# Two-layer trunk on one core: head transposes as SBUF-to-SBUF block moves and a VectorE block transpose, in place of TensorE transposes

## The chip, the cores and the metric

The kernel runs on one core of a Trainium2 chip. The metric is the device time of one execution in microseconds (us), the median of three runs.

## The reference, cut to what matters

The residual stream x has 256 positions of 2048 values, in float32. Two layers are computed one after the other.

```
even layer: h = rms_norm(x); proj = h @ w_in               # 2048 -> 32 heads x (q, k, v, gate) x 128
  heads 0-15  (stick-breaking): z = q k^T / sqrt(128), strict causal mask;
              A = exp(log_sigmoid(z) + reverse cumulative sum of log_sigmoid(-z));  o = A v
  heads 16-31 (dilated): q, k rms-normed per head; three dilated causal softmaxes merged;  o = P v
  x = x + (o * silu(gate)) @ w_out                         # 4096 -> 2048
odd layer: h = rms_norm(x); proj = h @ w_in                # 32 heads x (q, forget, input, gate) x 128
  HGRN2 per head: S_t = diag(f_t) S_{t-1} + (1 - f_t) i_t^T;  o_t = S_t^T q_t
  x = x + (rms_norm(o) * silu(gate)) @ w_out
```

In the score product of a head, and in the output product that takes up the gated outputs (`mix`), the 128 values of a head are summed over. TensorE sums over partitions, so queries, keys and `mix`, which come out with positions on partitions, have to be turned.

## The kernel before, in words

Each of the 64 heads is a product of the 256 positions with 2048 x 512 weights (128 columns each of q, k, v and gate). `product` runs over 16 steps of 128 rows; a step is six matmuls of 128x512 (two halves of the positions, and three terms each: high part of x times high part of the weights, high times low, low times high; lines L254 to L256). Two steps share one weight pair: `Feed.load` (L200) brings 512 KB into one of four buffers `raw`, ScalarE casts it to the high part `whi` (L211), VectorE subtracts to get the low part `wlo` (L212). `whi` and `wlo` have four buffers each, so a head takes eight pairs, and up to four pairs can stand split ahead of TensorE (`AHEAD`). After a layer's 32 heads, four output products of 32 steps read the turned `mixh` and `mixl` in the same way.

The work of a head behind its product is a generator (`stick_breaking`, `dilated` or `hgrn`). `Side.tick` moves the generators on once per step of the next heads' products; a `yield n` means "go on n steps later". So side work of one head lies between the matmuls of the next two. A tile scheduler then places all of this into one fixed order per engine. It may put an instruction later than the source has it when its own estimate says that the inputs are not there yet. Each engine, and the queue of SyncE (SP) that issues the transfers, runs its list strictly in order.

The generator starts with `evacuate` (L275): ScalarE copies the two 128x512 accumulators out of PSUM, scaled. These copies have to wait for the last matmul of the head. `flip` (L137) turns 128x128 blocks on TensorE against an identity matrix, into PSUM: four per head for queries and keys (`flip_pair`), two for the gated outputs (`emit_mix`), and three for attention weights in the even layer (`flip_weights`, not changed). In `emit_mix`, `split_into` (L128, L129) writes the turned `mixh` and `mixl` straight from PSUM.

Of the kernel before, what the change touches and what calls it, by code (L numbers as in the profile page):

```python
# [18 lines left out]
P = 128  # L19
# [15 lines left out]
def hybrid_trunk(  # L35
# [34 lines left out]
    ones = const.tile([P, SEQ], F32, name="ones")  # L70
    nc.vector.memset(ones, 1.0)
# [68 lines left out]
    def flip_pair(pj):  # L140

        ps = flip([pj[:, t, c * P : (c + 1) * P] for c in range(2) for t in range(NT)])
        return ps.rearrange("p (c t) -> p c t", c=2)
# [134 lines left out]
    def gate_exp(pj):  # L278

        g = pj[:, :, 384:512]  # L280
# [14 lines left out]
    def weighted_values(at0, at1, at11, pj, c):  # L295


        o = psb.tile([P, NT, P], F32, name="att")
        v = pj[:, :, c * P : (c + 1) * P]
        nc.tensor.matmul(o[:, 0, :], at0, v[:, 0, :], start=True, stop=True)  # L300
        nc.tensor.matmul(o[:, 1, :], at1, v[:, 0, :], start=True, stop=False)  # L301
        nc.tensor.matmul(o[:, 1, :], at11, v[:, 1, :], start=False, stop=True)  # L302
        return o

    def stick_breaking(h, pj):
        sg = gate_exp(pj)
        yield 4
        ps = flip_pair(pj)
        qk = work.tile([P, 2, SEQ], F32, name="qk", bufs=2)
        nc.scalar.copy(qk, ps)  # L310
        yield 3
        zp = psb.tile([P, 384], F32, name="att")
        nc.tensor.matmul(zp[:, 0:128], qk[:, 0, 0:P], qk[:, 1, 0:P], start=True, stop=True)  # L313
        nc.tensor.matmul(zp[:, 128:384], qk[:, 0, P:], qk[:, 1, :], start=True, stop=True)  # L314
# [10 lines left out]
        for lo, hi in ((0, 128), (128, 384)):  # L325
            back = sp[:, lo:hi][:, ::-1]
            nc.vector.tensor_tensor_scan(back, ones[:, 0 : hi - lo], back, 0.0, ALU.mult, ALU.add)
# [5 lines left out]
        o = weighted_values(at[:, 0:128], at[:, 128:256], at[:, 256:384], pj, 2)  # L333
        nc.vector.tensor_mul(sg, o, sg)
        yield 2
        emit_mix(h, sg, 1.0)

    def dilated(h, pj):
        sg = gate_exp(pj)
        qv = pj[:, :, 0:256].rearrange("p t (c d) -> p t c d", c=2)  # L340
# [7 lines left out]
        for t in range(NT):  # L348
            sl = pj[:, t, P : 2 * P]
# [7 lines left out]
        z = psb.tile([P, 384], F32, name="att")  # L357
        nc.tensor.matmul(z[:, 0:128], qk[:, 0, 0:P], qk[:, 1, 0:P], start=True, stop=True)  # L358
        nc.tensor.matmul(z[:, 128:384], qk[:, 0, P:], qk[:, 1, :], start=True, stop=True)  # L359
# [22 lines left out]
        o = weighted_values(at[:, 0:128], at[:, 128:256], at[:, 256:384], pj, 2)  # L382
# [5 lines left out]
        emit_mix(h, sg, 1.0)  # L388

    def hgrn(h, pj):  # L390
        g = pj[:, :, 384:512]
# [8 lines left out]
        nc.scalar.activation(f, fp, AF.Sigmoid)  # L400
# [3 lines left out]
        nc.scalar.activation(kk, fp, AF.Sigmoid, scale=-1.0)  # L404
        q = work.tile([P, SEQ], F32, name="qt", bufs=2)
        nc.scalar.copy(q, ps[:, 0, :])
        nc.scalar.activation(kk, kk, AF.Copy, scale=oml[:, h : h + 1])

        def blocks(a, n):
            return a.rearrange("p (b n) -> p b n", n=n)  # L410
# [24 lines left out]
        nc.vector.tensor_mul(qb, q, qb)  # L435
# [7 lines left out]
        nc.vector.tensor_mul(qq, q, f)  # L443
# [77 lines left out]
        o = weighted_values(at[:, 0, :], cross, at[:, 1, :], pj, 2)  # L521
# [14 lines left out]
        emit_mix(h, sg, hg[:, 2:3])  # L536
# [13 lines left out]
    def head(layer, h, acc):  # L550
        pj = evacuate(acc, rstds[layer])
        if layer == 1:
            yield from hgrn(h, pj)
        elif h < NSB:
            yield from stick_breaking(h, pj)
        else:
            yield from dilated(h, pj)
# [143 lines left out]
```

## Time and profile before

| quantity | value |
|---|---|
| median of three runs | 1967.46 us (1967.27 to 1967.49) |
| profiled execution, its own time | 1967.47 us |
| its span on the core | 1965.7 us |
| TensorE busy | 1956.2 us (100%) |
| VectorE busy | 1286.5 us (65%) |
| ScalarE busy | 1038.3 us (53%) |
| DMA, share of 16 engines | 54%, 175 GB/s in the mean |
| granted TensorE clock | 1.00 |

The span is what the trace covers; the time of the profiled execution is 1.8 us longer. Busy time of TensorE counts a pipelined matmul to its modelled end, so two matmuls overlap in it: a 128x512 matmul shows 0.39 us, but the next one starts 0.23 us after it.

### The profile page before, as it was taken

Reading aid. Unit: us, or ns where it says so; the run is one execution under the profiler, and the core shown is the slowest. Engines: PE = TensorE matmul, PEld = TensorE weight load, DVE = VectorE, ACT = ScalarE, POOL = GpSimd, SP = SyncE. Lnnn points to the kernel's source line nnn. Section 1 sums busy time; section 2 is a strip of 40 time slices with the busy share of each in tenths; the row PEclk is TensorE's granted clock in tenths of the full one; section 3 lists DMA queues with packets and bytes.
Section 4 is the critical chain, followed back from the end, with each engine's and each line's share of the span. In section 5 each row is a group of like instructions: output and inputs, shape, how many; then the busy total and the mean of one; then the engine's idle time right before and its main releaser. Section 6 shows DMA issues by size and latency. Waiting matters only on the chain.

```text
span 1965.7 us, 25693 instructions
## 1 busy us (share of the span) xinstructions
PE 1956.2 (100%) x9280; PEld 1611.5 (82%) x9280; DVE 1286.5 (65%) x2456; ACT 1038.3 (53%) x1653; POOL 55.9 (3%) x54
## 2 busy tenths in 40 slices
PE   8999999999999999999999999999999999999999
PEld 7888888888888888888888888888888888888887
DVE  6666666666666666555577777777777777776444
ACT  6555555555555555444455555555555555555432
POOL 0000000000000000000000000000000000000000
PEclk9999999999999999999999999999999999999999
DMA  9555555555555555555554544555555544455664
GB/s 324 166 178 175 173 174 177 173 172 175 177 173 173 175 176 172 181 183 192 187 177 161 162 160 161 172 161 165 166 163 162 165 162 160 158 169 164 200 204 139
DMA packets 97407, 344.39 MB, mean 175 GB/s; under 512 B 11136, under 2 KB 12288, under 8 KB 97280
## 3 DMA queue, kind: packets, MB, share of 16 engines
q1 hardware_dynamic: 97136, 342.73, 54.0%
q8 instruction: 73, 1.20, 0.2%
q14 instruction: 54, 0.44, 0.1%
q10 hardware_dynamic: 144, 0.02, 0.0%
HBM read 340.61 MB, written 2.10 MB: 174 GB/s over the span
## 4 chain that ended last, share of the span: by engine, by line
PE 100%; DMA 0%; ACT 0%; DVE 0%; DVEq 0%; issue 0%
PE acc L254 30%; PE acc L256 30%; PE acc L255 30%; PE att L137 3%; PE att L461 2%; PE att L490 1%; PE att L301 1%; PE att L302 1%; PE att L300 1%; PE att L518 0%; PE att L359 0%; PE att L314 0%; DMA gn<-in_gains 0%; PE att L313 0%; PE att L358 0%; ACT xh L128 0%
## 5 line engine op out<-in xcount | busy, mean ns | idle before, releaser
L212 DVE TENSOR_TENSOR wlo<-raw,whi 128x1024 fp32r<-128x1024 f32 (+1 forms) x642 | 782.2, 1219 | 545.2 <-ACT whi L211 543.8
L211 ACT CAST whi<-raw 128x1024 fp32r<-128x1024 f32 (+1 forms) x642 | 673.2, 1049 | 631.6 <-PE acc L256 547.2
L254 PE MATMUL acc<-whi,xh 128*128 128x512 f32 x2048 | 837.4, 409 | 5.8 <-ACT whi L211 5.8
L256 PE MATMUL acc<-whi,xl 128*128 128x512 f32 x2048 | 802.6, 392 | 0.0
L255 PE MATMUL acc<-wlo,xh 128*128 128x512 f32 x2048 | 800.1, 391 | 0.0
L256 PEld LDWEIGHTS acc<-whi,xl 128*128 128x128 f32 x2048 | 384.9, 188 | 84.9
L254 PEld LDWEIGHTS acc<-whi,xh 128*128 128x128 f32 x2048 | 385.7, 188 | 79.0 <-ACT whi L211 5.8
L255 PEld LDWEIGHTS acc<-wlo,xh 128*128 128x128 f32 x2048 | 386.3, 189 | 72.0 <-DVE wlo L212 0.6
L254 PE MATMUL acc<-whi,mixh 128*128 128x512 f32 x512 | 201.8, 394 | 0.0
L256 PE MATMUL acc<-whi,mixl 128*128 128x512 f32 x512 | 199.5, 390 | 0.0
L255 PE MATMUL acc<-wlo,mixh 128*128 128x512 f32 x512 | 199.3, 389 | 0.0
L256 PEld LDWEIGHTS acc<-whi,mixl 128*128 128x128 f32 x512 | 96.1, 188 | 20.3
L255 PEld LDWEIGHTS acc<-wlo,mixh 128*128 128x128 f32 x512 | 96.2, 188 | 19.4
L254 PEld LDWEIGHTS acc<-whi,mixh 128*128 128x128 f32 x512 | 96.2, 188 | 19.3
L275 ACT ACTIVATE pj<-acc,rstd 128x512 f32<-128x512 f32 x128 | 87.5, 685 | 30.6 <-PE acc L256 30.1
L285 DVE RECIPROCAL sg<-sg 128x256 f32<-128x256 f32 x32 | 56.0, 1749 | 0.5
L179 POOL TENSOR_TENSOR rr<-rv,mhalf 128x4 f32<-128x4 f32 x16 | 29.3, 1833 | 716.0 <-DVE rv L178 716.0
L179 POOL TENSOR_TENSOR ro<-rv,mhalf 128x2 f32<-128x2 f32 x32 | 25.0, 780 | 831.0 <-DVE pr L474 808.0
L504 ACT COPY ri<-qk 128x128 f32<-128x128 f32 x32 | 9.6, 299 | 58.4 <-DVE qk L413 58.4
L137 PE MATMUL att<-ident,pj 128*128 128x128 f32 x256 | 38.5, 272 | 0.0
L413 DVE TENSOR_TENSOR qk<-qk 128x128 f32<-128x128 f32 x128 | 37.0, 289 | 2.2
L429 DVE RECIPROCAL ri<-qk 128x160 f32<-128x160 f32 x32 | 36.7, 1148 | 0.0
(141 smaller groups left out, 1272.3 us busy)
## 6 DMA issues: line engine op xcount, KB each, us to landing
raw<-in_w_odd SPq DMA_DIRECT2D x256, 512.0 KB, 3.6
raw<-in_w_even SPq DMA_DIRECT2D x254, 512.0 KB, 3.5
raw<-in_w_out SPq DMA_DIRECT2D x128, 512.0 KB, 3.5
xres<-in_xt SPq DMA_DIRECT2D x8, 256.0 KB, 7.3
xres<-in_x SPq DMA_DIRECT2D x4, 512.0 KB, 7.3
out<-xres SPq DMA_DIRECT2D x6, 256.0 KB, 5.1
raw<-in_w_even SPq DMA_DIRECT2D x4, 256.0 KB, 4.8
out<-xres SPq DMA_DIRECT2D x4, 128.0 KB, 2.0
```

The source lines that it names most:

```text
L137: nc.tensor.transpose(ps[:, i * P : (i + 1) * P], b, ident)
L179: nc.gpsimd.tensor_tensor(dst, v[:, 0:n], mhalf[:, 0:n], op=ALU.pow)
L211: nc.scalar.copy(hi[:, s, :], half[:, s, :])
L212: nc.vector.tensor_sub(lo[:, s, :], half[:, s, :], hi[:, s, :].bitcast(F32))
L254: nc.tensor.matmul(acc[t], sh[:, k, s], hi, start=(k == 0), stop=False)
L255: nc.tensor.matmul(acc[t], sh[:, k, s], lo, start=False, stop=False)
L256: nc.tensor.matmul(acc[t], sl[:, k, s], hi, start=False, stop=(k == nk - 1))
L275: nc.scalar.activation(pj[:, t, :], acc[t], AF.Copy, scale=rstd[:, t : t + 1])
L285: nc.vector.reciprocal(sg, sg)
L413: nc.vector.tensor_tensor(o, a, b.broadcast_to(list(o.shape)), op=ALU.mult)
L429: nc.vector.reciprocal(ri, f8[:, :, 3:8])
L461: nc.tensor.matmul(ps[:, t, :], kt[:, t * P : (t + 1) * P], qt[t], start=True, stop=True)
```

## The change

Queries and keys are evacuated into a tile of their own (`qkp`), values and gate into another (`pj`), with four 128x256 ScalarE instructions in place of two of 128x512. For all but the last head of a layer, `move_blocks` copies the tile to a second one (`mvp`, or `mvm` for `mix`) with 16 SBUF-to-SBUF transfers on SP's queue, one for each pair of 32-partition groups; 32x32 blocks change place, in runs of 128 bytes. Then one VectorE instruction (`turn_blocks`, STREAM_TRANSPOSE) turns each 32x32 block, back into the tile it came from. Between the two stands a `yield 4`. The last head of a layer keeps the TensorE transposes (of `qkp` with a copy from PSUM). The score products read `qkp` (`products`), the dilated head scales k in place, HGRN reads q and forget from SBUF, and `split_into` reads `mix` from SBUF. The scan in `stick_breaking` reads a broadcast column instead of a 128x256 tile of ones.

```
+    def move_blocks(src, name):
+        n = src.shape[2] // P
+        moved = work.tile([P, NT, n, 4, 32], F32, name=name, bufs=1)
+        to = moved.rearrange("p t c a j -> p (t c) a j")
+        v = src.rearrange("p t (c f) -> p (t c) f", f=P)
+        for a in range(4):
+            for b in range(4):
+                nc.sync.dma_start(
+                    to[32 * b : 32 * b + 32, :, a, :], v[32 * a : 32 * a + 32, :, 32 * b : 32 * b + 32]
+                )
+        return moved
+    def turn_blocks(dst, moved):
+        nc.vector.transpose(dst, moved.rearrange("p t c a j -> p (t c a j)"))
+    def turn_pair(qk, quick):
+        if quick:
+            ps = flip([qk[:, t, c * P : (c + 1) * P] for t in range(NT) for c in range(2)])
+            nc.scalar.copy(qk, ps.rearrange("p (t f) -> p t f", t=NT))
+        else:
+            moved = move_blocks(qk, "mvp")
+            yield 4
+            turn_blocks(qk.rearrange("p t f -> p (t f)"), moved)
...
     def evacuate(acc, rstd):
-        pj = work.tile([P, NT, 512], F32, name="pj", bufs=2)
-        for t in range(NT):
-            nc.scalar.activation(pj[:, t, :], acc[t], AF.Copy, scale=rstd[:, t : t + 1])
-        return pj
+        qk = work.tile([P, NT, 256], F32, name="qkp", bufs=2)
+        vg = work.tile([P, NT, 256], F32, name="pj", bufs=2)
+        for dst, c in ((qk, 0), (vg, 256)):
+            for t in range(NT):
+                nc.scalar.activation(
+                    dst[:, t, :], acc[t][:, c : c + 256], AF.Copy, scale=rstd[:, t : t + 1]
+                )
+        return qk, vg
...
     def emit_mix(h, mix, scale):
+        if h == NH - 1:
+            turned = flip([mix[:, t, :] for t in range(NT)])
+        else:
+            moved = move_blocks(mix, "mvm")
+            yield 4
+            turned = mix.rearrange("p t f -> p (t f)")
+            turn_blocks(turned, moved)
         mixed.append(h)
-        split_into(mixh[:, h, :], mixl[:, h, :], flip([mix[:, t, :] for t in range(NT)]), scale)
+        split_into(mixh[:, h, :], mixl[:, h, :], turned, scale)
...
-    def stick_breaking(h, pj):
-        sg = gate_exp(pj)
-        yield 4
-        ps = flip_pair(pj)
-        qk = work.tile([P, 2, SEQ], F32, name="qk", bufs=2)
-        nc.scalar.copy(qk, ps)
+    def stick_breaking(h, qk, vg):
+        sg = gate_exp(vg)
+        yield 2
+        yield from turn_pair(qk, False)
         yield 3
...
-        yield 8
-        ps = flip_pair(pj)
-        qk = work.tile([P, 2, SEQ], F32, name="qk", bufs=2)
-        nc.scalar.copy(qk[:, 0, :], ps[:, 0, :])
-        nc.scalar.activation(qk[:, 1, :], ps[:, 1, :], AF.Copy, scale=qkg)
+        yield 5
+        yield from turn_pair(qk, h == NH - 1)
+        k = qk[:, :, P:]
+        nc.scalar.activation(k, k, AF.Copy, scale=qkg)
         yield 3
...
-        yield 3
-        ps = flip_pair(pj)
-        fp = ps[:, 1, :]
+        yield 2
+        yield from turn_pair(qk, h == NH - 1)
+        q, fp = qk[:, :, 0:P], qk[:, :, P:]
```

The scheduler's order around the new instructions differs from the order before at many places. Three of them are shown, with the buffer numbers of the tiles, since they tell which head a row belongs to. The new file has other line numbers: the cast is L234 there, the low part L235, the evacuation L300, the gate L309 to L313, the turn L155.

First place, the end of a stick-breaking head's product. ScalarE before, where `acc_751` and `acc_752` are the finished head's accumulators, and `whi_891` (a row ahead of these), `whi_909` and `whi_927` the next head's first three weight pairs:

```order
L211 CAST whi_909<-raw_804 128x1024
L211 CAST whi_927<-raw_829 128x1024
L275 ACTIVATE pj_957<-acc_751,rstd0_429 128x512
L211 CAST whi_947<-raw_866 128x1024
L275 ACTIVATE pj_957<-acc_752,rstd0_429 128x512
L283 ACTIVATE sg_960<-sg_960 128x256
L211 CAST whi_974<-raw_889 128x1024
```

ScalarE now, where `acc_1236` and `acc_1237` are the finished head's accumulators, `whi_1348` is its last pair, `whi_1385` the next head's first pair and `whi_1420` its second:

```order
L234 CAST whi_1348<-raw_1238 128x1024
L234 CAST whi_1385<-raw_1268 128x1024
L300 ACTIVATE qkp_1471<-acc_1236,rstd0_429 128x256
L300 ACTIVATE pj_1472<-acc_1236,rstd0_429 128x256
L300 ACTIVATE qkp_1471<-acc_1237,rstd0_429 128x256
L300 ACTIVATE pj_1472<-acc_1237,rstd0_429 128x256
L310 ACTIVATE sg_1477<-sg_1477 128x256
L234 CAST whi_1420<-raw_1303 128x1024
```

Before, three pairs of the next head are cast ahead of the first copy out of the finished accumulators; now one is, and the second is cast behind all four copies and the gate's exponential. VectorE at the same place before (`wlo_948` is the next head's fourth pair):

```order
L212 TENSOR_TENSOR wlo_928<-raw_829,whi_927 128x1024
L212 TENSOR_TENSOR wlo_948<-raw_866,whi_947 128x1024
L282 TENSOR_SCALAR sg_960<-pj_957 128x256
L284 TENSOR_SCALAR sg_960<-sg_960 128x256
L285 RECIPROCAL sg_960<-sg_960 128x256
L212 TENSOR_TENSOR wlo_975<-raw_889,whi_974 128x1024
```

VectorE now (`wlo_1386` belongs to the next head's first pair, `wlo_1421` to its second; `qkp_1250` is the tile of the head before the finished one, `att_1369` its scores):

```order
L235 TENSOR_TENSOR wlo_1386<-raw_1268,whi_1385 128x1024
L309 TENSOR_SCALAR sg_1477<-pj_1472 128x256
L311 TENSOR_SCALAR sg_1477<-sg_1477 128x256
L312 RECIPROCAL sg_1477<-sg_1477 128x256
L155 STREAM_TRANSPOSE qkp_1250<-mvp_1280 128x512
L313 TENSOR_TENSOR sg_1477<-sg_1477,pj_1472 128x256
L354 SCALAR_TENSOR_TENSOR wt_1372<-att_1369,strict_89 128x384
L235 TENSOR_TENSOR wlo_1421<-raw_1303,whi_1420 128x1024
```

The low part of the second pair has moved behind the gate, the turn of the older head's queries and keys, and the read of its scores.

Second place, the middle of a stick-breaking head. ScalarE before, around the copy of a head's turned outputs (`mixh`):

```order
L211 CAST whi_1060<-raw_945 128x1024
L320 ACTIVATE qv_1049<-wt_1047 128x384
L321 ACTIVATE qv_1049<-qv_1049 128x384
L128 ACTIVATE mixh_108<-att_1070 128x256
L322 ACTIVATE qv_1049<-qv_1049 128x384
L211 CAST whi_1083<-raw_972 128x1024
```

ScalarE now, where `atk_1325` are the turned weights of the head whose output `weighted_values` makes next, `sg_811` is an older head's `mix` and `whi_1305` the running head's sixth pair:

```order
L234 CAST whi_1270<-raw_1162 128x1024
L367 ACTIVATE wt_1151<-wt_1151 128x384
L172 COPY atk_1325<-att_1321 128x384
L128 ACTIVATE mixh_108<-sg_811 128x256
L234 CAST whi_1305<-raw_1197 128x1024
```

The cast of the sixth pair now stands behind `mixh`, which waits for the turn of `sg_811` on VectorE; there that turn stands behind the gating of the output just made (`L372`, it reads the result of `weighted_values`).

Third place, the end of an HGRN head's product. ScalarE before, where `whi_14300` is the next head's third pair:

```order
L211 CAST whi_14300<-raw_14185 128x1024
L504 COPY ri_14296<-qk_14134 128x128
L275 ACTIVATE pj_14338<-acc_14071,rstd1_7882 128x512
L211 CAST whi_14320<-raw_14215 128x1024
L275 ACTIVATE pj_14338<-acc_14072,rstd1_7882 128x512
```

ScalarE now, where `whi_13638` is the finished head's last pair, `whi_13668` and `whi_13686` are the next head's first two, and `qkp_13501` is the turned tile of the head before the finished one:

```order
L234 CAST whi_13638<-raw_13467 128x1024
L234 CAST whi_13668<-raw_13516 128x1024
L300 ACTIVATE qkp_13775<-acc_13465,rstd1_8783 128x256
L300 ACTIVATE pj_13776<-acc_13465,rstd1_8783 128x256
L300 ACTIVATE qkp_13775<-acc_13466,rstd1_8783 128x256
L300 ACTIVATE pj_13776<-acc_13466,rstd1_8783 128x256
L431 ACTIVATE sg_13781<-pj_13776 128x256
L438 ACTIVATE qk_13599<-qkp_13501 128x256
L442 ACTIVATE qk_13599<-qkp_13501 128x256
L443 ACTIVATE qk_13599<-qk_13599,oml_98 128x256
L234 CAST whi_13686<-raw_13562 128x1024
```

Here too one pair is cast ahead of the copies, where three were, and the second now stands behind three instructions that need the older head's turn.

## Rows read from the trace of the kernel before

**Rows 1.** The page, busy time of each engine.

```profile
PE 1956.2 (100%) x9280; PEld 1611.5 (82%) x9280; DVE 1286.5 (65%) x2456; ACT 1038.3 (53%) x1653; POOL 55.9 (3%) x54
```

**Rows 2.** Waits: engine, line, waited for: us in total, times, longest.

```profile
ACT whi L211 <- PE acc L256: 547.2, 427, 2.4
...
PE acc L254 <- ACT whi L211: 5.8, 1, 5.8
```

**Rows 3.** Timeline of ScalarE around a stick-breaking boundary: start, us, what, [idle before].

```profile
295.39 0.69 ACT L275 ACTIVATE pj<-acc,rstd 128x512 f32<-128x512 f32 x1 [0.99 <-PE acc L256]
296.07 1.05 ACT L211 CAST whi<-raw 128x1024 fp32r<-128x1024 f32 x1
297.02 0.68 ACT L275 ACTIVATE pj<-acc,rstd 128x512 f32<-128x512 f32 x1
298.62 0.42 ACT L283 ACTIVATE sg<-sg 128x256 f32<-128x256 f32 x1 [0.91 <-DVE sg L282]
```

**Rows 4.** The chain that ended last, by line, share of the span.

```profile
by line: PE acc L254 30.5%; PE acc L256 29.9%; PE acc L255 29.7%; PE att L137 2.8%; PE att L461 1.8%; PE att L490 1.2%; PE att L301 0.7%; PE att L302 0.7%; PE att L300 0.7%; PE att L518 0.4%; PE att L359 0.4%; PE att L314 0.4%; DMA gn<-in_g
```

**Rows 5.** Timeline of TensorE in the dilated heads.

```profile
601.27 0.40 PE L254 MATMUL acc<-whi,xh 128*128 128x512 f32 x1
...
603.55 0.39 PE L255 MATMUL acc<-wlo,xh 128*128 128x512 f32 x1
...
604.69 0.38 PE L358 MATMUL att<-qk 128*128 128x128 f32 x2
604.91 0.60 PE L359 MATMUL att<-qk 128*128 128x256 f32 x2
605.15 0.58 PE L254 MATMUL acc<-whi,xh 128*128 128x512 f32 x1
```

**Rows 6.** Timeline of VectorE in the same head as rows 3.

```profile
297.15 1.23 DVE L212 TENSOR_TENSOR wlo<-raw,whi 128x1024 fp32r<-128x1024 f32 x1 [1.50 <-ACT whi L211]
...
299.07 0.29 DVE L284 TENSOR_SCALAR sg<-sg 128x256 f32<-128x256 f32 x1 [0.48 <-ACT sg L283]
299.39 1.75 DVE L285 RECIPROCAL sg<-sg 128x256 f32<-128x256 f32 x1
...
307.32 0.42 DVE L334 TENSOR_TENSOR sg<-att,sg 128x256 f32<-128x256 f32 x1
309.15 0.56 DVE L316 SCALAR_TENSOR_TENSOR wt<-att,strict 128x384 f32<-128x384 f32 x1 [1.41 <-PE att L314]
```

**Rows 7.** Timeline of ScalarE in an HGRN head.

```profile
1324.55 0.38 ACT L400 ACTIVATE qk<-att 128x256 f32<-128x256 f32 x1
1324.82 0.38 ACT L404 ACTIVATE qk<-att 128x256 f32<-128x256 f32 x1
```

**Rows 8.** Groups by line and shape: count, busy us, mean ns, idle before.

```profile
L128 ACT ACTIVATE mixh<-att 128x256 fp32r<-128x256 f32 x32 | 12.3, 384 | 9.3 <-PE att L137 9.3
...
L342 DVE TENSOR_TENSOR sp<-pj 128x512 f32<-128x512 f32 x16 | 11.0, 685 | 0.0
...
L384 DVE SCALAR_TENSOR_TENSOR sg<-att,ws,sg 128x128 f32<-128x128 f32 x32 | 9.7, 344 | 0.0
...
L355 ACT ACTIVATE qk<-att,qkg 128x256 f32<-128x256 f32 x16 | 7.7, 482 | 0.0
...
L365 DVE CUSTOM_DVE_ANT_0 sp<-att,bias 128x256 f32<-128x256 f32 x16 | 6.7, 420 | 0.0
```

**Rows 9.** Timeline of SP's queue, transfers issued one behind the other.

```profile
16.48 0.42 SPq L88 DMA_DIRECT2D strict<-in_cmask  x1
16.95 0.43 SPq L89 DMA_DIRECT2D bias<-in_cmask  x1
```

**Rows 10.** DMA queues, 0 to 5 us: packets, MB, share of 16 engines' time.

```profile
q10 hardware_dynamic: 144, 0.02, 2.3%
```

**Rows 11.** The page, DMA issues: count, KB each, median us to landing.

```profile
out<-xres SPq DMA_DIRECT2D x4, 128.0 KB, 2.0
```

**Rows 12.** One stretch of the odd layer: busy time by engine, granted clock, DMA share, GB/s.

```profile
1035.00:1770.00 735.00, 735.00 (x3591) 599.08 (x3591) 531.74 (x1310) 415.75 (x803) 22.12 (x28) 1.00 0.51 163
```

More of the change, by code (lines that the diff above doesn't have):

```diff
@@ L69, in hybrid_trunk @@
     lbr = const.tile([P, 2, NH], F32, name="lbr")
-    ones = const.tile([P, SEQ], F32, name="ones")
-    nc.vector.memset(ones, 1.0)
+    one = const.tile([P, 1], F32, name="one")
+    nc.vector.memset(one, 1.0)
     ident = const.tile([P, P], F32, name="ident")
@@ L303, in weighted_values, with products @@
         return o
-    def stick_breaking(h, pj):
-        sg = gate_exp(pj)
-        yield 4
-        ps = flip_pair(pj)
-        qk = work.tile([P, 2, SEQ], F32, name="qk", bufs=2)
-        nc.scalar.copy(qk, ps)
+    def products(qk):
+        ps = psb.tile([P, 384], F32, name="att")
+        k = qk[:, :, P:]
+        nc.tensor.matmul(ps[:, 0:128], qk[:, 0, 0:P], k[:, 0, :], start=True, stop=True)
+        nc.tensor.matmul(ps[:, 128:384], qk[:, 1, 0:P], k, start=True, stop=True)
+        return ps
+    def stick_breaking(h, qk, vg):
+        sg = gate_exp(vg)
+        yield 2
+        yield from turn_pair(qk, False)
         yield 3
-        zp = psb.tile([P, 384], F32, name="att")
-        nc.tensor.matmul(zp[:, 0:128], qk[:, 0, 0:P], qk[:, 1, 0:P], start=True, stop=True)
-        nc.tensor.matmul(zp[:, 128:384], qk[:, 0, P:], qk[:, 1, :], start=True, stop=True)
+        zp = products(qk)
         z = work.tile([P, 384], F32, name="wt", bufs=2)
@@ L326, in stick_breaking @@
             back = sp[:, lo:hi][:, ::-1]
-            nc.vector.tensor_tensor_scan(back, ones[:, 0 : hi - lo], back, 0.0, ALU.mult, ALU.add)
+            nc.vector.tensor_tensor_scan(back, one.broadcast_to([P, hi - lo]), back, 0.0, ALU.mult, ALU.add)
         nc.vector.tensor_sub(z, z, sp)
@@ L332, in stick_breaking, with dilated @@
         yield 3
-        o = weighted_values(at[:, 0:128], at[:, 128:256], at[:, 256:384], pj, 2)
+        o = weighted_values(at[:, 0:128], at[:, 128:256], at[:, 256:384], vg)
         nc.vector.tensor_mul(sg, o, sg)
         yield 2
[L336 to L340, printed above, removed]
+        yield from emit_mix(h, sg, 1.0)
+    def dilated(h, qk, vg):
+        sg = gate_exp(vg)
+        qv = qk.rearrange("p t (c d) -> p t c d", c=2)
         sq = work.tile([P, NT, 2, P], F32, name="sp", bufs=2)
@@ L348, in dilated @@
         for t in range(NT):
[L349 removed]
+            sl = qk[:, t, P:]
             nc.vector.tensor_scalar_mul(sl, sl, rr[:, 2 * t + 1 : 2 * t + 2])
[L351 to L355 removed]
+        yield 5
+        yield from turn_pair(qk, h == NH - 1)
+        k = qk[:, :, P:]
+        nc.scalar.activation(k, k, AF.Copy, scale=qkg)
         yield 3
[L357 to L359 removed]
+        z = products(qk)
         nm = small.tile([P, NT], F32, name="nm")
@@ L381, in dilated @@
         yield 3
-        o = weighted_values(at[:, 0:128], at[:, 128:256], at[:, 256:384], pj, 2)
+        o = weighted_values(at[:, 0:128], at[:, 128:256], at[:, 256:384], vg)
         for t in range(NT):
@@ L387, in dilated, with blocks, hgrn @@
         yield 2
-        emit_mix(h, sg, 1.0)
-    def hgrn(h, pj):
-        g = pj[:, :, 384:512]
+        yield from emit_mix(h, sg, 1.0)
+    def blocks(a, n):
+        return a.rearrange("p (b n) -> p b n", n=n)
+    def hgrn(h, qk, vg):
+        g = vg[:, :, P:]
         sg = work.tile([P, NT, P], F32, name="sg")
@@ L403, in hgrn @@
         )
-        nc.scalar.activation(kk, fp, AF.Sigmoid, scale=-1.0)
-        q = work.tile([P, SEQ], F32, name="qt", bufs=2)
-        nc.scalar.copy(q, ps[:, 0, :])
+        nc.scalar.activation(blocks(kk, P), fp, AF.Sigmoid, scale=-1.0)
         nc.scalar.activation(kk, kk, AF.Copy, scale=oml[:, h : h + 1])
-        def blocks(a, n):
-            return a.rearrange("p (b n) -> p b n", n=n)
         def times(o, a, b):
@@ L442, in hgrn @@
         qq, cross = qc[:, 0:SEQ], qc[:, SEQ:]
-        nc.vector.tensor_mul(qq, q, f)
+        nc.vector.tensor_mul(blocks(qq, P), q, blocks(f, P))
         qv = work.tile([P, 8, 48], F32, name="qv", bufs=2)
@@ L520, in hgrn @@
         yield 2
-        o = weighted_values(at[:, 0, :], cross, at[:, 1, :], pj, 2)
+        o = weighted_values(at[:, 0, :], cross, at[:, 1, :], vg)
         so = small.tile([P, NT], F32, name="so")
@@ L535, in hgrn @@
         yield 2
-        emit_mix(h, sg, hg[:, 2:3])
+        yield from emit_mix(h, sg, hg[:, 2:3])
     srcs = []
@@ L550, in head @@
     def head(layer, h, acc):
-        pj = evacuate(acc, rstds[layer])
+        qk, vg = evacuate(acc, rstds[layer])
         if layer == 1:
-            yield from hgrn(h, pj)
+            yield from hgrn(h, qk, vg)
         elif h < NSB:
-            yield from stick_breaking(h, pj)
+            yield from stick_breaking(h, qk, vg)
         else:
-            yield from dilated(h, pj)
+            yield from dilated(h, qk, vg)
     def residual(layer, n, acc, ssq):
```

15 lines of the change are left out of this document (6 added, 9 removed).

## The prediction

> **What bounds the kernel now.** I read the page first: TensorE is busy for the whole span [rows 1]. Busy time counts pipelined ends, so I checked the chain and the waits. In the chain the reader is to see TensorE at every step, 90% of it in the three matmul lines and 2.8% in the transposes of line L137 [rows 4]. In the waits the reader is to see which way the waiting goes: ScalarE waits 547.2 us for TensorE to give back `whi` buffers, and TensorE waited for a cast just once, for 5.8 us, at the start [rows 2]. So TensorE is the bound and never starves, because the weight pairs are split ahead of it. The timeline shows what keeps it so at the end of a head: a cast stands between the two copies of the accumulators [rows 3], and the order before has three further casts ahead of the first copy. TensorE then has three pairs in hand, while ScalarE and VectorE do the head's boundary work.
>
> **What the change removes.** 62 heads lose four and two transposes each, 372 of the 512 at L137 (480 of heads, 32 of the residual). The chain gives that line 2.8% of 1965.7 us, 55 us or 0.107 us each; 372 of them are 40 us, 0.65 us per head. That is all that TensorE can gain.
>
> **The moves.** 62 x 32 = 1984 transfers join SP's queue. Issued back to back, one follows the other after 0.47 us [rows 9]; 40 issues per head (8 weight loads) are 18.8 us, less than the 96 matmuls of a head, which take 96 x 0.228 = 21.9 us (0.228 is ten steps from 601.27 to 603.55 in rows 5). Packets: 16 x (128 + 64) runs of 128 bytes and about 512 completion packets, 3584 per head. The nearest row is a 128-byte-per-partition load: 144 packets in 2.3% of 16 x 5 us, 12.8 ns each [rows 10]; so 2.9 us per engine and head, beside a DMA share that is 0.51 now [rows 12]. The nearest landing time is 2.0 us [rows 11], so a batch of 16 takes 7.5 + 2 = 9.5 us. The scheduler has put the turn of `qkp` almost a head behind its moves (the turn at a boundary is that of the head before the finished one), so I cost the moves at nothing. Their cover is that distance, some 20 us; without it 9.5 us per batch would show.
> The Trainium skill, "DMA: Bandwidth & Descriptors", section "Rules for kernel authors", speaks against the change: transfers under 64 KB are mostly overhead and should be merged. Its fixed cost of about 2.0 us, paid in turn by 32 transfers, would be an estimated 64 us per head and some 4400 us in all; no row shows that such costs add up, and the issues 0.47 us apart speak against it.
>
> **VectorE and ScalarE.** The new VectorE transpose is in no row. Below it lies half of the 128x512 multiply's 0.69 us [rows 8], 0.34 us; above it the reciprocal's rate, 1.75 us for 256 columns [rows 6], 3.5 us for 512. I take 0.69, as an instruction that reads and writes each element once, and 0.42 for 256 columns. Small four-piece evacuations start 0.27 us apart and last 0.38 [rows 7], so ScalarE is no worse off in work. What matters is the order.
>
> **Where TensorE will wait.** Time 0 is the end of a head's last matmul. The next slot of TensorE lies 0.16 us before it (0.39 us long, 0.23 apart), a pair takes 12 x 0.228 = 2.74 us, so the next head's first pair is used up at 2.58. Each hand-over costs 0.03 us (cast 296.07 + 1.05, low part at 297.15 [rows 3, 6]).
>
> Stick-breaking boundary, 14 heads, one pair in hand (first place of the order). Copies of the second accumulator end at 0.03 + 0.27 + 0.38 = 0.68. Then gate: VectorE 0.29 (the row of L284 for the same shape), exponential 0.42, VectorE 0.29, reciprocal 1.75 [rows 3, 6]: 1.00, 1.45, 1.77, 3.55 with hand-overs. Turn 0.69: 4.27. Now TensorE can make the scores, whose last result comes 0.82 us after their start (604.69 to 605.51 [rows 5]): 5.1. L354, the old L316, 0.56 [rows 6]: 5.7. Only then the second pair's low part, 1.23: 6.95. TensorE would want it at 2.58 + 0.46 (scores) + 0.46 (two matmuls with `whi` alone) = 3.50. It waits 3.45 us.
> Middle of the same head (second place). From the end of `weighted_values` (result 0.17 after its slot) run gating 0.42, turn 0.42, `mixh` 0.38, cast 1.05, low part 1.23 and five hand-overs, 3.84 us, against six matmuls of the fifth pair and two of the sixth, 1.83: 2.0 us of waiting. In between, VectorE's rows in order bring the exponentiated weights about 0.4 us late for their transposes. Together 5.85 us per head.
>
> Dilated boundary, 15 heads, two pairs in hand. Turn at 4.27, k scaled 0.48 [rows 8]: 4.8; scores inside the second pair, result at 5.65; two masked maxima, about 0.85 (2 x 0.42, rows 8): 6.5; third pair's low part 7.75, wanted at 2.58 + 2.74 + 0.46 + 0.46 = 6.25: 1.5 us. Weights' transposes about 0.5. Middle: the gating is two instructions of 0.34 [rows 8] and no matmuls of the fifth pair are left to cover it: 4.0 - 0.46 = 3.5 us. Together 5.5.
>
> HGRN boundary, 28 heads, one pair in hand (third place). Copies 0.68, sigmoid 0.42, a VectorE multiply 0.42, turn 0.69: 2.3. Then two sigmoids 0.27 apart, a copy of 0.5, the cast 1.05: 4.55, low part 5.8; wanted at 2.58 + 0.46 = 3.05: 2.75 us. The score matmuls further on now follow each other within 5 steps instead of 9, about 0.5 us more. Together 3.25.
>
> The first three heads and the first four of the odd layer keep three or more pairs and get no wait in this sum. **Sum:** 14 x 5.85 + 15 x 5.5 + 28 x 3.25 - 40 = 81.9 + 82.5 + 91 - 40 = 215 us. The profiled execution's own time is 1967.47 us (span 1965.7 and 1.8 around it), equal to the median; I forecast **2180 us**.
>
> Bounds: transposes at 0.34 take 0.35 x 57 + 0.21 x 29 = 26 us off; independent rows overlap by some 0.1 us, and the smaller waits (0.4 to 0.5 per head, 26 us in all) may vanish: about 2100. Transposes at the reciprocal's rate add 2.8 x 57 + 1.3 x 29 = 197 us: 2380, and I hold the upper half of that unlikely, as the multiply is the nearer row. The likeliest case's own range is 2095 to 2290.
>
> **Rivals.**
> Not slower: the boundary work is short enough for one pair. Place: between the end of a head's product and the second low part. For it speaks that before the change this work never stopped TensorE; against it that three pairs covered it then. It decides where the chain of 6.95 us falls to 3.50, for which the gate's reciprocal and the turn would have to cost nothing. Time: 1967 - 40 = 1927 us. Chance 0.05.
> The moves become the bound: SP in its order would hold back the weight loads. With stalls a stick-breaking head takes about 96 x 0.228 + 1.5 + 5.85 = 29.2 us, so a move has to cost more than (29.2 - 8 x 0.47) / 32 = 0.8 us on SP. Issues of up to 512 KB cost 0.47, which speaks against it; for it, that no row shows a transfer between SBUF tiles or eight of them in flight. At 1.0 us each a head takes 32 + 3.8 = 35.8 us; 62 heads: at least 62 x 6.6 us more, about 2600. The skill's rule on small transfers points this way. Chance 0.12.
> TensorE's clock falls in the new gaps. The clock is granted at 1.00, the 2.4 GHz level, in every stretch that I read [rows 12], but TensorE hardly stops there, so the rows say nothing of gaps of 2 to 3 us. If after one gap per head one pair ran at half speed, that is 2.74 us x 57 = 156 us: 2335. The Trainium skill, "TensorE: Matmul & The Clock Gate", section "Why this matters for your kernels", says that idle gaps between bursts of matmuls bring the clock to its lower level; by that rule this case is met if the gaps are long enough, which no row here shows. Chance 0.13.
>
> **How the numbers follow.** Forecast 0.70, clock 0.13, moves 0.12, not slower 0.05. The forecast's range and the clock case hold 0.83, so the range reaches from 2095 to 2340. Within 0.2% is about what a measurement can tell from no change; no case lies there, and I leave it 0.01. Slower gets 0.94, faster 0.05.
>
> **What would show it.** Right: TensorE idle some 270 us in all, waiting for low parts on VectorE and casts, two gaps in even heads and one in odd ones, heads of 29 us (even) and 28 (odd); the four 256-wide copies ahead of the second cast; 372 transposes gone; VectorE never waiting for moves. Wrong: TensorE's chain passing through SP or DMA, the turn waiting for transfers, a granted clock under 1.00 in the layers, or gaps of another size at the three places.

## The result, and the profile after

| | median | range |
|---|---|---|
| before | 1967.37 us | 1967.19 to 1967.49 |
| after | 2297.34 us | 2290.74 to 2298.86 |
| ratio | 1.167 | 95% interval 1.165 to 1.169 |

The change costs 330 us. The time lies in the range of the prediction (2095 to 2340) on the side that it gave, 117 us above its point. It lies outside the range of the likeliest case by itself (2095 to 2290).

The page, busy time of each engine after the change; it answers to [rows 1].

```profile
PE 2059.2 (90%) x8908; PEld 1619.4 (71%) x8908; DVE 1343.5 (58%) x2580; ACT 1021.5 (44%) x1719; POOL 40.0 (2%) x54
```

372 matmuls are gone, and yet TensorE is busy longer: 10% of the span it is idle, and part of its matmuls are slower. The chain that ended last, by engine and by line, against [rows 4]:

```profile
PE 48%; SPq 19%; DMA 13%; DVE 9%; ACT 6%; issue 5%; DVEq 0%; POOL 0%; ACTq 0%; POOLq 0%
SPq L148 18%; PE acc L278 15%; PE acc L279 15%; PE acc L277 14%; DMA raw<-in_w_even 6%; DVE wlo L235 5%; DMA raw<-in_w_odd 4%; ACT whi L234 3%; DMA mvm<-sg 1%; SPq L223 1%; PE att L494 1%; ACT pj L300 1%; DVE qkp L155 1%; PE att L523 1%; ACT qkp L300 1%
```

TensorE has lost half of the chain, and the issue of the moves on SP (L148) holds 18% of it. The waits (us in total, times, longest), against [rows 2]:

```profile
ACT whi L234 <- PE acc L279: 280.2, 173, 2.5
...
PE acc L277 <- ACT whi L234: 148.4, 62, 6.0
...
PE acc L278 <- DVE wlo L235: 54.9, 74, 1.8
ACT whi L234 <- DMA raw<-in_w_odd: 53.8, 88, 2.3
...
ACT whi L234 <- DMA raw<-in_w_even: 52.9, 73, 4.1
```

TensorE now waits for casts and low parts, 136 times in place of once, and ScalarE waits half as long for TensorE. But casts also wait for weights (`raw`), which the forecast did not have. SP's queue in two HGRN heads shows why:

```profile
1551.63 8.00 SPq L223 DMA_DIRECT2D raw<-in_w_odd  x6
1559.68 10.82 SPq L148 DMA_DIRECT2D mvm<-sg  x16
1570.60 1.00 SPq L223 DMA_DIRECT2D raw<-in_w_odd  x2
1571.66 10.24 SPq L148 DMA_DIRECT2D mvp<-qkp  x16
1582.01 8.06 SPq L223 DMA_DIRECT2D raw<-in_w_odd  x6
```

A batch of 16 moves takes 10.2 us of SP, 0.64 us per move. Two batches stand almost side by side, so in 22 us only two of a head's eight weight loads go out.

The turn is in the list of groups (count | busy us, mean ns | idle before):

```profile
L155 DVE STREAM_TRANSPOSE qkp<-mvp 128x512 f32<-128x512 f32 x62 | 42.6, 687 | 30.6 <-DMA mvp<-qkp 30.2 <-issue 0.3
L155 DVE STREAM_TRANSPOSE sg<-mvm 128x256 f32<-128x256 f32 x62 | 27.3, 440 | 7.9 <-DMA mvm<-sg 7.4 <-DMA mvp<-qkp 0.3
```

### The profile page after: what moved, and what is told of

It reads as the page before. It is cut to its first block, busy times and chain, and to the rows that moved or that the text cites. A ratio compares the mean times of both kernels' runs of the same rounds, so it can differ in the third digit from the quotient of the medians.

```text
span 2296.9 us, 27640 instructions
## 1 busy us (share of the span) xinstructions
PE 2059.2 (90%) x8908; PEld 1619.4 (71%) x8908; DVE 1343.5 (58%) x2580; ACT 1021.5 (44%) x1719; POOL 40.0 (2%) x54
## 4 chain that ended last, share of the span: by engine, by line
PE 48%; SPq 19%; DMA 13%; DVE 9%; ACT 6%; issue 5%; DVEq 0%; POOL 0%; ACTq 0%; POOLq 0%
SPq L148 18%; PE acc L278 15%; PE acc L279 15%; PE acc L277 14%; DMA raw<-in_w_even 6%; DVE wlo L235 5%; DMA raw<-in_w_odd 4%; ACT whi L234 3%; DMA mvm<-sg 1%; SPq L223 1%; PE att L494 1%; ACT pj L300 1%; DVE qkp L155 1%; PE att L523 1%; ACT qkp L300 1%
## 5 line engine op out<-in xcount | busy, mean ns | idle before, releaser
L235 DVE TENSOR_TENSOR wlo<-raw,whi 128x1024 fp32r<-128x1024 f32 (+1 forms) x642 | 774.5, 1218 | 313.5 <-ACT whi L234 303.5
L278 PE MATMUL acc<-wlo,xh 128*128 128x512 f32 x2048 | 856.8, 418 | 53.6 <-DVE wlo L235 52.9
L234 ACT CAST whi<-raw 128x1024 fp32r<-128x1024 f32 (+1 forms) x642 | 661.3, 1043 | 414.9 <-PE acc L279 280.2
L279 PE MATMUL acc<-whi,xl 128*128 128x512 f32 x2048 | 837.5, 409 | 0.0
L277 PEld LDWEIGHTS acc<-whi,xh 128*128 128x128 f32 x2048 | 398.2, 197 | 247.1 <-ACT whi L234 166.4
L278 PEld LDWEIGHTS acc<-wlo,xh 128*128 128x128 f32 x2048 | 407.0, 199 | 178.0 <-DVE wlo L235 97.0
L279 PEld LDWEIGHTS acc<-whi,xl 128*128 128x128 f32 x2048 | 406.6, 199 | 82.5 <-issue 0.2
L300 ACT ACTIVATE qkp<-acc,rstd 128x256 f32<-128x256 f32 x128 | 60.7, 475 | 246.5 <-PE acc L279 246.5
L309 DVE TENSOR_SCALAR sg<-pj 128x256 f32<-128x256 f32 x32 | 9.4, 293 | 130.6 <-ACT pj L300 130.6
L432 DVE TENSOR_TENSOR sg<-sg,pj 128x256 f32<-128x256 f32 x32 | 13.6, 425 | 104.1 <-ACT sg L431 104.0
L128 ACT ACTIVATE mixh<-sg 128x256 fp32r<-128x256 f32 x31 | 12.9, 418 | 125.5 <-DVE sg L155 125.5
L300 ACT ACTIVATE pj<-acc,rstd 128x256 f32<-128x256 f32 x128 | 60.7, 475 | 0.0
L155 DVE STREAM_TRANSPOSE qkp<-mvp 128x512 f32<-128x512 f32 x62 | 42.6, 687 | 30.6 <-DMA mvp<-qkp 30.2
L372 DVE TENSOR_TENSOR sg<-att,sg 128x256 f32<-128x256 f32 x16 | 6.8, 425 | 83.1 <-PE att L336 83.0
```

Of the source, the lines that this page charges most:

```text
L155: nc.vector.transpose(dst, moved.rearrange("p t c a j -> p (t c a j)"))
L234: nc.scalar.copy(hi[:, s, :], half[:, s, :])
L235: nc.vector.tensor_sub(lo[:, s, :], half[:, s, :], hi[:, s, :].bitcast(F32))
L277: nc.tensor.matmul(acc[t], sh[:, k, s], hi, start=(k == 0), stop=False)
L278: nc.tensor.matmul(acc[t], sh[:, k, s], lo, start=False, stop=False)
L279: nc.tensor.matmul(acc[t], sl[:, k, s], hi, start=False, stop=(k == nk - 1))
```

## The experiments

Theory 1 is the prediction's: the order leaves too few weight pairs in hand, and TensorE waits for casts and low parts behind boundary work. Its first rival, called theory 2 below, is SP's queue: the moves hold back weight loads and turns. The second is the clock in the gaps.

Head lengths below are read from the timeline, from one head's first copy out of the accumulators to the next head's. Line numbers in the experiments' rows are those of their own files, a few lines off.

**Casts first.** In the changed kernel a head's work is issued behind the last cast and low part that the source has split by then (`issue_after` ties everything traced inside it behind one instruction of the same engine, as an order and not as a wait). The order then has four pairs in hand at the end of nearly every head. (`feed.last` holds the last cast and low part; the lines that fill it are left out here.)

```
-                side.tick()
+                with tc.issue_after(feed.last[0].ins), tc.issue_after(feed.last[1].ins):
+                    side.tick()
```

> The changed kernel with all its 32 moves per head on SP's queue and the same arithmetic, but what a head's boundary issues on ScalarE and VectorE now stands behind the casts and low parts of the weight pairs that the source has split by then: four pairs in hand at the end of every head, as in the kernel before. Theory 1, the order of casts against boundary work is the cause: TensorE's waits for casts and low parts go (248 us of waits of the accumulators for ScalarE and VectorE fall under 40), and what is left is bounded by TensorE (1967 - 40 = 1927 us) or by SP with 32 x 0.64 + 8 x 0.47 = 24.2 us per head against some 23.4 of TensorE, about 50 us more in all: 1930 to 2000 us. Rival, SP's in-order queue is the cause: nothing there changes, the HGRN heads keep their 30.8 us, and the time stays above 2200. Rival, slower clock in the gaps: it follows the gaps, granted clock back to 0.99 or more if theory 1 holds.

Measured: 2268.35 us (ratio 1.153, 1.151 to 1.154). Theory 1 alone fails: with the pairs back in order the loss stays, and TensorE waits 195 us for casts and low parts, against 203 us in the rows above (the 248 us of the expectation are not in them). The rows of its waits and of its chain say where it went:

```profile
DVE qkp L155 <- DMA mvp<-qkp: 286.2, 60, 6.5
...
ACT whi L235 <- DMA raw<-in_w_even: 238.1, 153, 9.2
...
SPq 34%; PE 30%; DMA 20%; DVE 8%; issue 5%; ACT 3%; DVEq 0%; POOL 0%; ACTq 0%; POOLq 0%
```

Casts wait for weights that stand behind moves on SP, and the turn waits for its moves with low parts queued behind it on VectorE.

**Moves on GpSimd's queue**, and **half of the change** either way:

```
-                nc.sync.dma_start(
+                nc.gpsimd.dma_start(
```
```
-        if h == NH - 1:                  # gated outputs through TensorE in every head
+        if True:
```
```
-        if quick:                        # queries and keys through TensorE in every head
+        if True:
```

> The changed kernel with the same 32 moves per head issued by GpSimd in place of SP, and nothing else edited. The order that results has three or four pairs in hand at the end of each head again. Theory 1 (order): 1925 to 1975 us, TensorE waiting under 60 us for casts and low parts. Rival, SP's queue: the same, since SP then holds only weight loads; so this run does not tell these two apart, but it tells both from a third, that the moves themselves (their 3584 packets per head beside the weights, or the turns and small evacuations on VectorE and ScalarE) cost the time: then it stays above 2200. If GpSimd needs over 0.75 us per move it becomes the bound (24 us per head), at 1.0 us 32 us per head and about 2500.

> Half of the change: queries and keys by moves and a turn, gated outputs by TensorE transposes as before, so 16 moves per head on SP and 124 TensorE transposes come back. The order has three or four pairs in hand in all heads but the third. Theory 1 (order): no gaps, 1967 - 248 x 0.107 = 1940 us, within 1930 to 1965; theory 2 (SP, 16 x 0.64 + 3.8 = 14 us per head): no gaps either, unless the turn waits for its moves. If each move carried a share of the loss of 330 us, two thirds of the moved bytes would bring about 165 us or more: above 2100.

> The other half: gated outputs by moves and a turn, queries and keys by four TensorE transposes and a copy. 16 moves per head on SP, 124 TensorE transposes gone. The order has three or four pairs in hand in all heads. Theory 1: 1967 - 124 x 0.107 = 1954 us, within 1945 to 1980 (the copy of queries and keys now covers 512 columns on ScalarE in the HGRN heads too, where two sigmoids read the accumulator before). If each move carried a share of the loss: 2080 to 2150.

Measured: 2152.59 us (1.093, 1.092 to 1.095), 1992.35 us (1.0128, 1.0113 to 1.0143) and 1981.38 us (1.0071, 1.0056 to 1.0086). The first misses both marks: GpSimd takes 0.55 us of its own for each move, and VectorE waits 355 us for moves in front of turns (for `mvp` 166.9 before `qkp` and 86.7 before `sg`, for `mvm` 43.4 and 58.0). TensorE there waits only 6.8 us for casts and low parts, but 151 us for the heads' own work, 89 of them in front of score products whose queries and keys come late. The halves keep three or four pairs in hand and lose little, but they don't gain, and both lie above their marks of 1930 to 1965 and 1945 to 1980. The loss is no price per move: half of the issues bring 25 and 14 us of the 330, or 52 and 27 with the transposes saved (248 and 124 x 0.107) counted in.

**The order without the moves.** Both theories had now one run against them, so the next pair takes the moves out. In the first kernel ScalarE, VectorE and TensorE are held to the changed kernel's order, instruction by instruction; in the second the boundary work stands behind the casts.

```
-        moved = work.tile([P, NT, n, 4, 32], F32, name=name, bufs=1)
...
-                nc.sync.dma_start(
...
+        moved = still if n == 2 else still1        # zeros, written once
...
+    pin_order(tc)                                  # first of the two only
```

> The changed kernel with ScalarE, VectorE and TensorE each held to the changed kernel's own order, row for row (one weight pair in hand at the end of the stick-breaking and HGRN heads, two in the dilated ones), but the 32 moves per head are left out: the turns read a buffer of zeros, so queries, keys and gated outputs are not those of the inputs. SP issues weight loads alone. Theory 1 of the prediction (that order by itself starves TensorE): its sum stands unchanged, 2180 us, within 2100 to 2290. Theory 2, formed after the run with casts first (the 32 moves stand in SP's queue almost in one piece of 21 us with two weight loads between them, so the raw weights come late, and the scheduler's order only mirrors that lateness): TensorE's waits for casts and low parts nearly vanish and the time is that of TensorE, 1927 to 1960 us.

> The same without the 32 moves (turns of a buffer of zeros), but with the boundary work behind the casts as in the first run, so four pairs in hand. Both theories: what TensorE alone needs, 1927 us, within 1920 to 1945. The difference to the run with the changed kernel's order is the price of the order by itself: some 250 us by theory 1, under 30 by theory 2.

Measured: 2239.88 us (1.138, 1.137 to 1.140) and 1923.35 us (0.978, 0.976 to 0.979). So the order alone costs 316.5 us, and theory 2, that it only mirrors late weights, falls. A stick-breaking head of the first of the two, TensorE's timeline:

```profile
316.09 0.39 PE L299 MATMUL acc<-whi,xl 128*128 128x512 f32 x1
318.21 0.49 PE L363 MATMUL att<-qkp 128*128 128x128 f32 x2 [1.72 <-DVE qkp L175]
...
318.78 0.82 PE L297 MATMUL acc<-whi,xh 128*128 128x512 f32 x2
320.91 0.79 PE L298 MATMUL acc<-wlo,xh 128*128 128x512 f32 x1 [1.31 <-DVE wlo L255]
321.50 0.63 PE L299 MATMUL acc<-whi,xl 128*128 128x512 f32 x1
321.93 0.63 PE L298 MATMUL acc<-wlo,xh 128*128 128x512 f32 x1
...
333.84 0.40 PE L299 MATMUL acc<-whi,xl 128*128 128x512 f32 x1
335.09 0.73 PE L297 MATMUL acc<-whi,xh 128*128 128x512 f32 x2 [0.86 <-ACT whi L254]
336.35 0.50 PE L298 MATMUL acc<-wlo,xh 128*128 128x512 f32 x1 [0.53 <-DVE wlo L255]
```

The first pair ends with the slot at 316.09. With the next slot 0.23 later, the scores and two matmuls with `whi` (0.46 each), the low part is wanted at 317.24. It is taken at 320.91, a wait of 3.67 us where the forecast had 3.45. In the middle it is wanted at 333.84 + 0.23 + 0.46 = 334.53 and taken at 336.35, 1.82 against 2.0. Behind the two idle stretches of this boundary, 1.72 and 1.31 us, the matmuls follow each other after 0.43 us and not 0.23. The windows of the same kernel give the granted clock there (third column from the right: 0.50 is the 1.2 GHz level):

```profile
318.20:321.00 2.80, 1.48 (x7) 0.99 (x7) 1.95 (x3) 1.24 (x2) 0.00 (x0) 0.95 0.00 0
321.00:324.10 3.10, 3.10 (x8) 2.42 (x9) 2.72 (x3) 2.94 (x5) 0.00 (x0) 0.50 0.59 186
324.10:334.00 9.90, 9.90 (x49) 8.10 (x47) 3.59 (x7) 1.32 (x3) 0.00 (x0) 1.00 0.44 156
```

**Moves spread out**, and **two queues with late turns.**

```
+            yield 2                                # spread: after every four moves, on SP
```
```
+        queue = nc.gpsimd if name == "mvp" else nc.sync
...
             moved = move_blocks(qk, "mvp")
-            yield 4
+            yield 9                                # the same for "mvm"
...
-        if h == NH - 1:                            # in emit_mix, both kernels
+        if h >= NH - 2:
```

> The first run (boundary work behind the casts) with the 16 moves of a batch issued four at a time, two steps of the product apart, so that a weight load stands between every four or eight moves on SP's queue; the gated outputs of the last two heads of a layer go through TensorE. SP still issues 24.2 us per head. Theory 2 (a batch holds the loads back): the pairs come in time and a head takes what SP or TensorE need, 24.2 to 25.5 us, 1970 to 2060 us. Rival, SP's whole issue time per head is the bound however it is spread, with its waits for free raw buffers on top: heads stay at 29 us or more, above 2200. Theory 1 says nothing here that the first run did not say.

> Boundary work behind the casts, moves of queries and keys on GpSimd's queue, those of gated outputs on SP's, and each turn nine steps of the product (12 us) behind its moves in place of four. SP issues 16 x 0.64 + 8 x 0.47 = 14 us per head, GpSimd 16 x 0.6 = 9.6. Theory 2: no load waits for long and no turn for its moves, so TensorE is the bound: 1927 to 1960 us, faster than the kernel before. Rival, the time from the first move to the last landing (9.6 + 3.3 = 12.9 us on GpSimd) keeps the turn and the low parts behind it waiting as in the run with all moves on GpSimd: 1990 to 2100 us.

Measured: 2153.43 us (1.095, 1.093 to 1.096) and 1926.62 us (0.9796, 0.9780 to 0.9813). Spreading gives 115 us back and not the 200 or more that I had expected; dilated heads fall to 26 us, HGRN heads stay at 29. So batches that hold loads back are part of what the moves cost. Casts still wait 446 us for weights there; whether the 24 us of issue that SP needs per head, whatever the spread, are the reason is not shown. Two queues with late turns beat both kernels, and their 32 moves cost 3 us beside the run without any (1923.35). The chain of that run is TensorE again, and it waited for a cast once:

```profile
PE 94%; DMA 2%; DVE 1%; ACT 1%; issue 1%; POOL 0%; SPq 0%; DVEq 0%; ACTq 0%
...
PE acc L280 <- ACT whi L236: 5.7, 1, 5.7
DVE qkp L156 <- DMA mvp<-qkp: 5.1, 6, 2.3
```

**The gaps filled, and the parts of the good version undone.** The first of these four adds matmuls of a zero tile to the run that holds the order without the moves:

```
+                fill[last.name] = [
+                    nc.tensor.matmul(acc[1], nil, xh[:, 0:2, :], start=False, stop=False).ins
+                    for _ in range(n)
+                ]
```

The others are the version on two queues, in turn with all moves on SP (without the `queue` line), without `issue_after`, and with `yield 4` in place of 9 (there `emit_mix` is the changed kernel's too).

> The run without moves that holds the changed kernel's order (2239.9 us; same zeros in the turns), with one thing added: where TensorE stood idle at each boundary it gets matmuls of a zero tile that add nothing to the accumulator and wait for nothing, 7 in a stick-breaking head (gap of 1.72 us), 10 in a dilated one (2.44), 8 in an HGRN one (2.02), 0.228 us each. No needed work comes earlier, so the gaps of the order stay as long as they are. Clock rival of the prediction: behind each of these gaps eight or so matmuls follow each other after 0.43 us in place of 0.228, at a granted clock of 0.50; if the idle time is what lowers it, they come back to 0.228, 57 heads x 1.6 us = 91 us less: 2140 to 2175 us and a granted clock of 0.99 or more. If the clock does not hang on these gaps, or the short gap that is left (0.5 to 1.3 us) lowers it as well: 2230 to 2260.

> As the run on two queues (1926.6 us), but all 32 moves on SP's queue: boundary work behind the casts, turns nine steps behind the moves, gated outputs of the last two heads by TensorE. Against the first run (2268.4) it changes when the turns come. If the weight loads behind the moves in SP's queue are the cause there, it stays above 2200; if it was the turns that waited for their moves with low parts queued behind them (286 us of VectorE's waits in the first run), it comes to 1930 to 2000.

> As the run on two queues with turns nine steps behind the moves, but nothing holds the boundary work behind the casts: the order is the scheduler's own, which here has three or four pairs in hand again. Theory 1 in its present form (the order costs what it costs only where one or two pairs are in hand): 1925 to 1945 us, the same as with it within 1%. If holding the order mattered there: above 1960.

> Boundary work behind the casts and two queues, but each turn four steps (5.5 us) behind its moves as in the changed kernel. The moves of a batch need 9.6 + 3.3 us on GpSimd and 10.2 + 1.8 on SP to the last landing, so VectorE waits some 6 us in the turn with the low parts behind it; four pairs in hand last 11 us. If that covers it: 1925 to 1945. If not, 6 us twice per head less the cover: 1960 to 2100.

Measured: 2230.02 us (1.134, 1.132 to 1.136), 2317.94 us (1.179, 1.177 to 1.181), 1994.91 us (1.014, 1.013 to 1.016) and 2064.73 us (1.050, 1.048 to 1.051).

Filled gaps. The sum moved by only 10 us, to the edge of the second mark, but the head rows tell the three kinds apart. First copies of stick-breaking heads in ScalarE's timeline, four without the filling and three with it:

```profile
282.71 0.47 ACT L320 ACTIVATE qkp<-acc,rstd 128x256 f32<-128x256 f32 x1 [5.85 <-PE acc L299]
...
313.12 0.47 ACT L320 ACTIVATE qkp<-acc,rstd 128x256 f32<-128x256 f32 x1 [5.82 <-PE acc L299]
...
343.71 0.47 ACT L320 ACTIVATE qkp<-acc,rstd 128x256 f32<-128x256 f32 x1 [5.82 <-PE acc L299]
...
374.37 0.47 ACT L320 ACTIVATE qkp<-acc,rstd 128x256 f32<-128x256 f32 x1 [5.85 <-PE acc L299]
```

```profile
306.99 0.47 ACT L339 ACTIVATE qkp<-acc,rstd 128x256 f32<-128x256 f32 x1 [5.84 <-PE acc L310]
...
336.29 0.47 ACT L339 ACTIVATE qkp<-acc,rstd 128x256 f32<-128x256 f32 x1 [5.83 <-PE acc L310]
...
365.61 0.47 ACT L339 ACTIVATE qkp<-acc,rstd 128x256 f32<-128x256 f32 x1 [5.83 <-PE acc L310]
```

Heads of 30.4 to 30.7 us become heads of 29.3 (the six before them alternate between some 29.3 and 31.9 us without it). Over 13 stick-breaking heads that is 16 us. Three windows of the filled run, of stick-breaking, mostly dilated and HGRN heads, have the granted clock at 1.00, 0.96 and 1.00:

```profile
70.00:400.00 330.00, 300.80 (x1329) 234.72 (x1327) 182.70 (x238) 138.56 (x215) 0.00 (x0) 1.00 0.43 145
400.00:900.00 500.00, 453.09 (x1938) 358.48 (x1939) 279.71 (x492) 199.06 (x298) 14.10 (x14) 0.96 0.41 138
1190.00:2080.00 890.00, 859.41 (x3966) 670.76 (x3965) 596.52 (x1486) 437.31 (x900) 22.25 (x32) 1.00 0.44 147
```

In stick-breaking heads the idle time does lower the clock, and that costs 1.2 us per head in the mean. 27 HGRN heads go from 29.6 to 28.9 us in the mean, 20 us in all. In the dilated heads I had put the filling at the wrong place: the gap of 2.44 us stands some 9 us behind it, so it only added time, 21 us over 15 heads. (Two heads, one ahead of the 13 and one ahead of the 27, were filled without having that gap, and grew by 1.4 and 1.6 us.) The expected 91 us were too much in any case: where the clock was held up, a head gained 1.2 and 0.7 us in the mean and not 1.6.

The price per head also shows in the run without the filling, in heads that follow one another with the same gaps (0.94 or 0.95, 2.44 and 0.53 us in the first three, which are dilated; 2.02 and 0.53 in the other two, HGRN):

```profile
674.40:704.50 30.10, 26.19 (x110) 20.56 (x109) 17.20 (x32) 12.19 (x19) 1.01 (x1) 0.94 0.42 139
704.50:734.60 30.10, 26.19 (x110) 20.55 (x109) 17.20 (x32) 12.13 (x18) 1.01 (x1) 0.94 0.45 142
734.60:763.20 28.60, 24.69 (x110) 19.41 (x110) 17.20 (x32) 12.19 (x19) 1.01 (x1) 1.00 0.39 135
...
1572.80:1602.80 30.00, 27.45 (x121) 21.30 (x120) 19.30 (x48) 14.15 (x30) 0.70 (x1) 0.94 0.46 151
1602.80:1631.20 28.40, 25.85 (x121) 20.14 (x120) 19.25 (x48) 14.18 (x29) 0.70 (x1) 1.00 0.41 137
```

Here a head in which the clock falls takes some 1.6 us more than one in which it stays at 1.00. Nine of the last 13 dilated heads are of the longer kind, 14 us in all.

The other three show that the good version needs all its parts: one queue costs 391 us more, early turns 138 us, the scheduler's own order 68 us. One queue lands on its mark of above 2200: against the first run, turns wait less for their moves (182 us, 315 there), casts wait more for weights (509 us, 293 there), and the time is 50 us longer. So late turns alone gain nothing, and the weight loads behind the moves are what costs there. The last two miss their first marks (1925 to 1945) and land on their second. With the own order VectorE waits 161 us in front of turns, but TensorE barely waits for weight pairs in either run (9 and 6 us); it waits for the heads' own work, 46 us with the own order and 93 us with early turns. The longest of these, own order first, then early turns:

```profile
PE att L335 <- ACT atk L173: 24.6, 13, 4.1
...
PE att L346 <- ACT qkp L395: 36.1, 15, 4.4
PE att L346 <- DVE qkp L156: 32.6, 15, 3.9
```

L346 is the score product, L335 the product with the turned weights (`atk`). So pairs in hand are not enough. With early turns the late turns themselves stop TensorE, at the score product, which stands in its order. With the own order it is the turned weights that come late; what delays them there is not shown.

## Why the prediction was right, and where it was off

The measured time lies inside the range only because the range was stretched to 2340 for the clock rival taken by itself; the likeliest case ended at 2290. Three of the signs of being wrong came as well: the chain passes through SP and DMA, turns wait for transfers (37.6 us), and the clock is under 1.00. So that the range held is in part luck.

The runs split the 330 us:

| part | runs | measured | forecast |
|---|---|---|---|
| transposes gone, other small edits | casts first without moves - before | 1923.4 - 1967.2 = -43.9 | -40 |
| order | order without moves - casts first without moves | 2239.9 - 1923.4 = +316.5 | +255.4 |
| moves, beside that order | after - order without moves | 2297.3 - 2239.9 = +57.5 | 0 |

**What TensorE can gain**: right, to 4 us; the "not slower" rival's 1927 is what it takes without waits.

**The order as the cause**: right. The order of the changed kernel loses nearly all of the time without a single move. In it the boundary and the middle of a stick-breaking head wait 3.67 and 1.82 us (forecast 3.45 and 2.0), and with the clock held up a head takes 29.3 us (forecast 29.2). HGRN heads wait 2.02 + 0.53 = 2.55 us at the boundary (2.75) and take 28.4 us where the clock stays at 1.00 (forecast 28). In dilated heads the middle gap is 2.44 + 0.53 = 2.97 us (3.5) and another one 0.94 us (1.5).

**The turn**: 0.69 and 0.44 us (forecast 0.69 and 0.42), so the upper half of the range was not needed. The copies are longer than forecast, 0.47 against 0.38 us.

**The clock**: not a rival but a part. Forecast and rival are both true at once: the order brings the gaps, and in a stick-breaking head one of them brings eight matmuls at 0.50 of the clock. Its price was mis-sized: 1.4 to 1.6 us in most of the heads in which the clock falls, and it does not fall in every one, against 2.74 in each. That is 16 us in the stick-breaking and 20 in the HGRN heads by the filled gaps, and 14 us in the dilated heads by the heads side by side, some 50 us together. The Trainium skill, "TensorE: Matmul & The Clock Gate", section "Why this matters for your kernels", says that idle gaps between bursts of matmuls lower the clock; the filled gaps agree, 29.3 us per head against 30.4 to 30.7.

**The moves cost nothing**: this is the step that failed. Three things behind it were off. A move takes 0.64 us of SP and not 0.47. In SP's order two batches hold 22 us with two weight loads between them, so weights come late. A load itself also takes longer to land, 4.6 us in the odd layer against 3.6 before and 3.3 in the order without moves; in the even layer it takes 4.8 against 3.5, but 4.5 without moves too, so there the moves are hardly the reason. And turns of queries and keys wait for their moves (20 times, 30.2 us), nearly always in HGRN heads. The transfers as such are not the price, since on two queues the same 32 cost 3 us. Beside the order that is 57.5 us, since the same pairs are late for both reasons; by itself, with casts first, it is 2268.4 - 1923.4 = 345 us. So either cause is enough, and undoing one alone gives back 29 or 57.5 us of 374. The rival "moves become the bound" wanted over 0.8 us per move; it takes effect at 0.64 already, as I had asked only for SP's total and not for what stands behind a batch in its queue. The Trainium skill, "DMA: Bandwidth & Descriptors", section "Rules for kernel authors", holds that spreading transfers over several issuing engines saves only issue time; here that issue time decides, 2317.9 us on one queue against 1926.6 on two.

The prediction lies 117 us low for these two terms: 61 us in the order (some 50 of it the clock; the rest is not settled) and 57.5 us of moves. Why the scheduler gave the casts up with 32 moves on SP, and kept them first with 16, with none or with 32 on GpSimd, is not shown by any run; that its plan counts SP's issues is my guess.

## What to carry to other kernels

Ask of a transfer not only how long it takes but what stands behind it in its queue: 16 small ones are 10 us in which no weight load goes out. When two causes each suffice, undoing one shows almost nothing; take both away, then put each back by itself. The idea of the change was sound (41 us faster, 2.0%) once the moves had a second queue, the turns came nine steps behind their moves and not four, and the feed of the bound engine was held in front.

## What the runs showed that I had not expected

- A transfer of 8 or 16 KB between SBUF tiles takes 0.59 us of SP and 0.05 to the next, against 0.42 and 0.05 for a load of 128x384 [rows 9]; on GpSimd it takes 0.55 us, and lands after 2.9 to 3.7 us in place of 1.8.
- In a stick-breaking head the granted clock falls to 0.50 for some 3 us behind 1.72 and 1.31 us of idle time close together, and stays at 1.00 behind 0.86 and 0.53, and also where seven matmuls fill the 1.72 and the 1.3 us are left. The gaps alone do not decide it: with the same gaps it falls in two dilated heads and not in the third.
